# Mixer C's score products: from 128-row stacks of high and low parts to 64-row products of a head's two parts on the two halves of the array's rows

## Chip, cores and metric

The kernel runs on one core of one Trainium2 chip. The metric is the device time of one execution in microseconds; lower is better.

## What is computed

The reference is a two-layer encoder trunk on 1024 tokens of width 1024. Layer 0 mixes by dilated window attention (mixer A) and latent attention (mixer B), layer 1 by differential attention (mixer C). Each layer goes on with a normalisation, a gated feed-forward net with a convolution, and a gated embedding. The change touches mixer C alone, which for each of 8 heads computes two score matrices from two query and two key parts of width 64:

```python
def mixer_c(x, cos_c, sin_c, w_qkv, lam_params, subln, w_out, lambda_init):
    ...
    q = apply_rope(h[..., :C_QK].reshape(B, S, C_HEADS, 2, C_HEAD_DIM), ...)
    k = apply_rope(h[..., C_QK:2 * C_QK].reshape(B, S, C_HEADS, 2, C_HEAD_DIM), ...)
    v = h[..., 2 * C_QK:].reshape(B, S, C_HEADS, 2 * C_HEAD_DIM)
    ...
    s = jnp.einsum("bhcqd,bhckd->bhcqk", qi, kf) * (dh ** -0.5)
    a = jax.nn.softmax(s, axis=-1)
    return jnp.einsum("bhqk,bhkd->bhqd", a[:, :, 0] - lam * a[:, :, 1], vf)
```

The factor dh ** -0.5 is 0.125. The outputs are normalised by head and projected.

## The kernel before

All large products run on TensorE (PE) in the type fp32r. To keep precision, each operand is split into a high part h, which is the value rounded to fp32r, and a low part l, which is the rest; a product is then the sum h*h + h*l + l*h (`mm3`, lines 157 to 160). The high parts are mostly written by ScalarE (ACT) and the low parts by VectorE (DVE, `lo_part`, line 141). GpSimd (POOL) does the rotation of queries and keys (lines 229 to 236), some high parts of weights (line 138), and scalings.

Mixer C goes head by head, and in each head by 8 tiles of 128 queries, so 64 items (`ItemC`, line 815). While a head's items run, the next head is projected, one tile of tokens in each slot (`Block64.project`, line 526). The names in the trace are:

- `pp`: the projection of one token tile to 384 columns (queries, keys, values of one head), 24 matmuls on lines 158 to 160. ACT copies queries and keys to `nat` (line 541) and the values' high part to `v` (line 549), DVE writes the values' low part, POOL rotates `nat` and copies the queries to `q` (line 138).
- `kt`: the transposed keys of one tile (`keys`, line 555, one transpose for both parts). They become `ks`, which holds the high part of a key part in 64 rows and its low part in the other 64: two copies by ACT (line 562) and two subtractions by DVE (line 141), each of 64 rows.
- `qt`: the transposed queries of one tile (`query`, line 565). POOL writes each part twice side by side, PE transposes each of the two doubled parts, ACT multiplies by 0.125 and rounds (line 574), DVE writes the low part (line 575). This is done three items ahead (`prep`).
- `s`: the scores of one part, 128 queries by 1024 keys, in two PSUM banks (`scores`, line 578). Each of two key halves takes two matmuls of 128 rows: high queries against the stack of high and low keys, then low queries against it. There are two such buffers, `bufs=2` in `banks2`, so the two parts of an item hold both.
- DVE takes the negative maximum of each row (`nmx`, line 828); ACT writes the exponentials `e` and their sum `l` (line 438); DVE takes the reciprocal `r` (line 833) and multiplies it by minus lambda for the second part (line 834); POOL scales the first `e` (line 835); DVE adds the second, scaled, to it (line 836).
- `xt`: eight transposes of an item's `e` (line 163), split into `pth` by ACT (line 397) and `ptl` by DVE (line 141), two halves each. After each second item these meet the values in `av`, 24 matmuls.

The loop that sets the order in which this is written is `pipeline` (line 469): in slot i come the scores and softmax of item i + 1 (`a`), the preparation of item i + 3, the slot's step of the plan (a projected tile of the next head, which also transposes the tile before it), the value products of the item before (`c`), and the transposes of item i (`b`):

```python
            if i + 1 < n:
                items[i + 1].a()
            if i + 3 < n:
                items[i + 3].prep()
            plan.run(i, "mid")
```

A scheduler then fixes each engine's order from this and puts in the waits; on the chip each engine runs its own list strictly in that order. Exponentials, split probabilities, keys, values, queries and the transposed input share one pool of 36 buffers of 4 KB in each partition (`unit`, `runit`). Banks of PSUM for `pp`, `kt`, `qt`, `xt` and `av` come from four others (`bank`). In the last slot of a head the weights of the head after next are loaded and split (line 148, `wl`). While the last head's items run, the slots hold weights and products of the following stages (`last_plan`, line 918).

Of the kernel before, what the change touches and what calls it, by code (L numbers as in the profile page):

```python
# [11 lines left out]
AF = mybir.ActivationFunctionType  # L12
ALU = mybir.AluOpType
AX = mybir.AxisListType

P = 128
NT = 8
NK = 8
# [13 lines left out]
def tile_hybrid_encoder(  # L32
# [32 lines left out]
    nc = tc.nc  # L65
# [15 lines left out]
    def runit(s, shape):  # L81
        return unit(s, shape, F32R)

    class Region:

        def __init__(self, kb):
            self.cm = tc.tile_pool(name=nm("rg"), bufs={2: 16, 3: 8, 4: 6}[kb])
            self.pool = self.cm.__enter__()
# [23 lines left out]
    def mid1(s, shape, dt=F32, tag="nat"):  # L112
        return sm.tile(shape, dt, tag=tag, name=nm(s), bufs=3 if tag == "nat" else 2)
# [7 lines left out]
    def bank(s):  # L121
        return ps.tile([P, 512], F32, tag="b", name=nm(s), bufs=4)

    def banks2(s):
        return ps.tile([P, 1024], F32, tag="s", name=nm(s), bufs=2)
# [4 lines left out]
    def blocks(ap):  # L130
        return ap.rearrange("p (k q) -> p k q", q=P)

    def tk(t):
        return slice((t % 4) * P, (t % 4) * P + P)
# [5 lines left out]
    def lo_part(lo, src, hi):  # L140
        nc.vector.tensor_tensor(lo, src, f32(hi), op=ALU.subtract)  # L141
# [15 lines left out]
    def mm3(o, lh, ll, rh, rl, start, stop):  # L157
        nc.tensor.matmul(o, lhsT=lh, rhs=rh, start=start, stop=False)  # L158
        nc.tensor.matmul(o, lhsT=lh, rhs=rl, start=False, stop=False)  # L159
        nc.tensor.matmul(o, lhsT=ll, rhs=rh, start=False, stop=stop)  # L160

    def transpose(o, i):
        nc.tensor.transpose(o, in_=i, identity=ident)  # L163
# [12 lines left out]
    C2a = cp.tile([P, NT, 16], F32, name="C2a")  # L176
# [260 lines left out]
    def exp_rows(dst, s, negmax, l):  # L437
        nc.scalar.activation(dst, s, AF.Exp, bias=negmax, scale=1.0, accum_out=l)  # L438
# [57 lines left out]
    class Block64:  # L496
# [29 lines left out]
        def project(self, t, lag=1):  # L526
            hf = t // 4
            if t % 4 == 0:
                self.ks[hf] = runit("ks", [P, 2, 512])
                self.v[hf] = runit("v", [P, 4, 256])  # L530
                if hf == 0:
                    self.q = unit("q", [P, NT, 2, 64])
            pp = bank("pp")
            for k in range(NK):
                xh, xl = self.xt.tok(k, t)
                wh, wl = self.w[k // 2]
                mm3(pp[:, 0:384], xh, xl, wh[:, k % 2, :], wl[:, k % 2, :], k == 0, k == NK - 1)
            if t >= lag:
                self.keys(t - lag)
            nat = mid1("nat", [P, 4, 64])  # L540
            nc.scalar.copy(nat, pp[:, 0:256].rearrange("p (j d) -> p j d", j=4))
            vt = self.v[hf][:, t % 4, :]
            if self.is_a:
                psv = pp[:, 256:384].rearrange("p (j d) -> p j d", j=2)
                vh = vt.rearrange("p (b d) -> p b d", d=64)[:, 0::3, :]
                vl = vt[:, 64:192].rearrange("p (b d) -> p b d", d=64)
            else:
                psv, vh, vl = pp[:, 256:384], vt[:, 0:128], vt[:, 128:256]
            nc.scalar.copy(vh, psv)
            lo_part(vl, psv, vh)  # L550
            rope(nat[:, :, 0:16], nat[:, :, 0:16], C2a[:, t, :], S2a[:, t, :], 4, 8)
            pool_copy(self.q[:, t], nat[:, 0:2, :])
            self.nat[t] = nat

        def keys(self, t):
            nat = self.nat.pop(t)
            pt = bank("kt")[:, 0:P]
            transpose(pt, nat[:, 2:4, :].rearrange("p j d -> p (j d)"))
            for j in range(2):
                h, l = (slice(0, 64), slice(64, 128)) if j == 0 else (slice(64, 128), slice(0, 64))  # L560
                ks = self.ks[t // 4][:, j, tk(t)]
                nc.scalar.copy(ks[h], pt[h])
                lo_part(ks[l], pt[h], ks[h])
# [11 lines left out]
            nc.vector.scalar_tensor_tensor(qt[:, 1], pt[:, 0:n, :], 0.125, f32(qt[:, 0]), op0=ALU.mult, op1=ALU.subtract)  # L575
            return qt

        def scores(self, qt, i, j):
            s = banks2("s")
            for kh in range(2):  # L580
                for hl in range(2):
                    nc.tensor.matmul(s[:, kh * 512:kh * 512 + 512], lhsT=qt[:, hl, i, :], rhs=self.ks[kh][:, j, :],  # L582
                                     start=hl == 0, stop=hl == 1)
            return s

    class ItemA:
        def __init__(self, blk, j, t, mask, st):
            self.blk, self.j, self.t, self.mask, self.st = blk, j, t, mask, st
# [151 lines left out]
    class Latent:  # L740
# [62 lines left out]
        def turn(self):  # L803
# [8 lines left out]
            nc.scalar.copy(h, pt[:, 0:kk, :])  # L812
            lo_part(l, pt[:, 0:kk, :], h)

    class ItemC:
        def __init__(self, blk, t, st):
            self.blk, self.t, self.st = blk, t, st

        def prep(self):
            self.qt = self.blk.query(self.t, [0, 1])  # L820

        def a(self):
            l = small("l2", [P, 2])
            es = []
            for j in range(2):
                s = self.blk.scores(self.qt, j, j)
                nmx = small("nmx", [P, 1])
                nc.vector.tensor_reduce(out=nmx, in_=s, axis=AX.X, op=ALU.max, negate=True)  # L828
                e = unit("e", [P, 1024])
                exp_rows(e, s, nmx, l[:, j:j + 1])  # L830
                es.append(e)
            r = small("r2", [P, 2])
            nc.vector.reciprocal(r, l)
            nc.vector.tensor_tensor(r[:, 1:2], r[:, 1:2], neglam, op=ALU.mult)
            nc.gpsimd.tensor_scalar(es[0], es[0], r[:, 0:1], 1.0, op0=ALU.mult, op1=ALU.mult)
            nc.vector.scalar_tensor_tensor(es[0], es[1], r[:, 1:2], es[0], op0=ALU.mult, op1=ALU.add)
            self.e = es[0]
# [173 lines left out]
    def mixer_c(xt, late):  # L1011
        new_region(3)
        oT2 = big("oT2", [P, 2, 1024])
        last = {}

        def sink(i):
            def f(oT):
                if i < 7:
                    nc.sync.dma_start(out=mix[1][i], in_=oT)
                last["oT"] = oT  # L1020
            return f
        blk = [Block64(xt, w_c[i], False) for i in range(8)]
        blk[0].load(True)
        for t in range(NT):
            blk[0].project(t, 2)
            if t == 1:
                late()
        blk[0].keys(NT - 2)
        items, plan = [], Plan()
        for i in range(8):  # L1030
            sti = {"sink": sink(i), "oT": oT2[:, i % 2, :] if i < 7 else unit("oT", [P, 1024])}
            items += [ItemC(blk[i], t, sti) for t in range(NT)]
            if i < 7:
                blk[i + 1].plan(plan, 8 * i - 1, 1)
            else:
                w, mt = last_plan(plan, 1, 56, 63)
        plan.add(-1, "first", lambda: blk[0].keys(NT - 1))
        plan.add(-1, "last", lambda: blk[1].load(True), lambda: blk[1].project(0))
        pipeline(items, plan)
        return w, mt, last["oT"]  # L1040
# [469 lines left out]
```

## Time and profile before

| what | value |
|---|---|
| runs | 3137.59, 3142.58 and 3142.8 us; median 3142.58 us |
| profiled execution | 3139.44 us, its span 3137.6 us, mean granted clock of TensorE 0.987 |
| busy, share of the span | PE 96%, weight loads of PE 83%, DVE 73%, ACT 38%, POOL 33% |
| chain that ended last | PE 82%, DVE 9%, DMA 3%, ACT 3%, issue 2%, POOL 2% |
| scores of mixer C, line 582 | 512 matmuls, 3.5% of the chain |

The profile is one execution, taken apart instruction by instruction. A row of a timeline gives start, length, engine, line, operation, the output and input by the program's names, their shapes, and in brackets how long the engine had been idle and what ended that. Matmuls overlap in the array, so the sum of their lengths is more than the time they take; the distance of their starts, or the chain of waits, gives what one costs in a row. A row that ends in "x2" joins two instructions in a row.

### The profile page before, as it was taken

The page shows a single profiled execution, that of the slowest core. Times are in us where ns is not written, and L with a number is a line of the kernel's source. Part 1 is how long each engine was busy: PE and PEld are TensorE (multiplying, and loading weights), DVE is VectorE, ACT ScalarE, POOL GpSimd, SP SyncE. Part 2 cuts the span into 40 slices and gives each one's busy share as a digit, 9 for nine tenths or more (in the row PEclk, how much of TensorE's full clock was granted, in tenths as well). Part 3 has the DMA queues.
Part 4 walks back from the last instruction along what each step waited for, and adds up shares of the span by engine and source line. Part 5 has one row for each costly group of instructions (what it writes and reads, how often), then busy time and mean ns, then how long its engine had stood idle before and what let it go on. Part 6 is the DMA issues. An engine that isn't in the chain of part 4 may idle for free.

```text
span 3137.6 us, 43123 instructions
## 1 busy us (share of the span) xinstructions
PE 3023.3 (96%) x15704; PEld 2590.5 (83%) x15704; DVE 2275.3 (73%) x3864; ACT 1182.2 (38%) x2502; POOL 1048.3 (33%) x1546
## 2 busy tenths in 40 slices
PE   8999999999799999999999999999888999999999
PEld 7888989888588888788889999998666888878887
DVE  6666487875887777766648777777679777767764
ACT  5555577761232222101225555555423222211111
POOL 4444534333422221101225555554333222201112
PEclk9999999999899999999999999999998999999999
DMA  3000100143122221623121100004322222244221
GB/s 119 28 28 25 31 28 8 36 131 124 67 81 81 86 84 67 226 101 108 54 68 31 35 28 28 28 18 134 103 99 68 81 81 81 81 167 141 101 74 67
DMA packets 89251, 237.52 MB, mean 76 GB/s; under 512 B 9040, under 2 KB 32720, under 8 KB 89040
## 3 DMA queue, kind: packets, MB, share of 16 engines
q1 hardware_dynamic: 89040, 234.76, 21.7%
q8 instruction: 125, 2.05, 0.3%
q14 instruction: 86, 0.70, 0.1%
HBM read 179.15 MB, written 55.57 MB: 75 GB/s over the span
## 4 chain that ended last, share of the span: by engine, by line
PE 82%; DVE 9%; DMA 3%; ACT 3%; issue 2%; POOL 2%; SPq 0%; DVEq 0%; ACTq 0%; POOLq 0%
PE pb L159 7%; PE pb L158 7%; PE pb L160 7%; PE xt L163 5%; PE pd L158 5%; PE pd L160 5%; PE pd L159 5%; PE pp L158 4%; PE pp L160 4%; PE pp L159 4%; PE s L582 3%; PE pa L158 3%; PE pa L160 2%; PE pa L159 2%; PE pg L158 2%
## 5 line engine op out<-in xcount | busy, mean ns | idle before, releaser
L158 PE MATMUL pd<-dh,dh 128*128 128x512 f32 x704 | 276.0, 392 | 8.5 <-ACT dh L324 7.5
L141 DVE TENSOR_TENSOR ptl<-xt,pth 128x512 fp32r<-128x512 f32 (+2 forms) x384 | 240.1, 652 | 57.8 <-ACT pth L397 41.3
L160 PE MATMUL pd<-dh,dl 128*128 128x512 f32 x704 | 275.1, 392 | 2.2 <-DVE dl L141 2.1
L1306 DVE TENSOR_TENSOR xn<-xn,pd 128x512 f32<-128x512 f32 x320 | 212.3, 684 | 88.5 <-PE pd L160 87.7
L159 PE MATMUL pd<-dl,dh 128*128 128x512 f32 x704 | 274.9, 391 | 0.0
L158 PE MATMUL pp<-wh,xth 128*128 128x384 f32 x768 | 266.4, 347 | 8.2 <-ACT wh L145 8.0
L159 PE MATMUL pp<-wl,xth 128*128 128x384 f32 x768 | 258.9, 337 | 1.3 <-DVE wl L148 1.3
L160 PE MATMUL pp<-wh,xtl 128*128 128x384 f32 x768 | 258.1, 336 | 0.0
L438 ACT ACTIVATE e<-s,nmx 128x1024 f32<-128x1024 f32 x192 | 214.4, 1118 | 96.6 <-DVE nmx L828 73.8
L158 PE MATMUL pb<-xt,wh 128*128 128x512 f32 x528 | 207.2, 392 | 0.0
L159 PE MATMUL pb<-xt,wh 128*128 128x512 f32 x528 | 206.9, 392 | 0.0
L160 PE MATMUL pb<-xt,wl 128*128 128x512 f32 x528 | 206.9, 392 | 0.0
L324 ACT CAST wh<-ws 128x512 fp32r<-128x512 f32 x132 | 81.7, 620 | 319.9 <-PE pb L159 261.8
L163 PE MATMUL xt<-ident,e 128*128 128x128 f32 x1440 | 194.7, 275 | 5.6 <-POOL e L731 3.0
L138 POOL TENSOR_SCALAR wh<-ws 128x512 fp32r<-128x512 f32 x44 | 29.8, 677 | 458.1 <-PE pa L159 428.8
L163 PEld LDWEIGHTS xt<-ident,e 128*128 128x128 f32 x1440 | 164.4, 141 | 18.7 <-POOL e L731 4.3
L141 DVE TENSOR_TENSOR wl<-ws,wh 128x512 fp32r<-128x512 f32 x176 | 160.8, 914 | 24.1 <-ACT wh L324 23.9
L324 ACT CAST dh<-dr 128x1024 fp32r<-128x1024 f32 x44 | 46.1, 1051 | 346.6 <-DMA dr<-gated 201.9
L138 POOL TENSOR_SCALAR dh<-dr 128x1024 fp32r<-128x1024 f32 x44 | 47.0, 1070 | 367.1 <-DMA dr<-in_w_down_dram 190.7
L158 PEld LDWEIGHTS pd<-dh,dh 128*128 128x128 f32 x704 | 132.9, 189 | 37.8 <-issue 8.3
L160 PEld LDWEIGHTS pd<-dh,dl 128*128 128x128 f32 x704 | 132.5, 188 | 32.9 <-DVE dl L141 5.3
L158 PEld LDWEIGHTS pp<-wh,xth 128*128 128x128 f32 x768 | 144.7, 189 | 13.8 <-ACT wh L145 8.9
(270 smaller groups left out, 8751.0 us busy)
## 6 DMA issues: line engine op xcount, KB each, us to landing
wf<-in_w_gate_dram SPq DMA_DIRECT2D x44, 512.0 KB, 3.2
wf<-in_w_up_dram SPq DMA_DIRECT2D x44, 512.0 KB, 4.2
gated<-c SPq DMA_DIRECT2D x44, 512.0 KB, 2.6
dr<-in_w_down_dram SPq DMA_DIRECT2D x44, 512.0 KB, 3.2
dr<-gated SPq DMA_DIRECT2D x44, 512.0 KB, 4.0
wr<-in_w_c_dram SPq DMA_DIRECT2D x32, 384.0 KB, 3.2
pes<-peo SPq DMA_DIRECT2D x64, 128.0 KB, 2.1
xmid<-xn SPq DMA_DIRECT2D x16, 512.0 KB, 2.9
```

Of the source, the lines that this page charges most:

```text
L138: nc.gpsimd.tensor_scalar(o, i, 1.0, 1.0, op0=ALU.mult, op1=ALU.mult)
L141: nc.vector.tensor_tensor(lo, src, f32(hi), op=ALU.subtract)
L158: nc.tensor.matmul(o, lhsT=lh, rhs=rh, start=start, stop=False)
L159: nc.tensor.matmul(o, lhsT=lh, rhs=rl, start=False, stop=False)
L160: nc.tensor.matmul(o, lhsT=ll, rhs=rh, start=False, stop=stop)
L163: nc.tensor.transpose(o, in_=i, identity=ident)
L324: nc.scalar.copy(h, v)
L438: nc.scalar.activation(dst, s, AF.Exp, bias=negmax, scale=1.0, accum_out=l)
L582: nc.tensor.matmul(s[:, kh * 512:kh * 512 + 512], lhsT=qt[:, hl, i, :], rhs=self.ks[kh][:, j, :], start=hl == 0, stop=hl == 1)
L1306: nc.vector.tensor_tensor(xns[t][:, sl], xns[t][:, sl], po, op=ALU.add)
```

## The change

Mixer C gets a block class of its own, `BlockC`. After the projection, one transpose turns both query parts of a tile and a second one both key parts, so that part 0 lies in rows 0 to 63 and part 1 in rows 64 to 127. ACT writes their high parts in one copy (line 841), DVE their low parts in one subtraction, into `qkh` and `qkl`, which each hold queries and keys of half the tokens. The doubled queries, their copies on POOL, and the queries' own transposes and splits are gone; `prep` is empty. The scores take, for each part and each half of the keys, three matmuls of 64 rows (high by high, high by low, low by high) instead of two of 128, twelve in all, in which the two parts alternate (line 851). The factor 0.125 moves from the query to the softmax: DVE multiplies the negative maximum by it (line 870), and the exponential has it as its scale (line 871).

```diff
+        def keys(self, t):
+            nat = self.nat.pop(t)
+            pt = blocks(bank("kt"))[:, 0:2, :]
+            for i in range(2):
+                transpose(pt[:, i, :], nat[:, 2 * i:2 * i + 2, :].rearrange("p j d -> p (j d)"))
+            h, l = (x[:, :, tk(t)] for x in self.qk[t // 4])
+            nc.scalar.copy(h, pt)
+            lo_part(l, pt, h)
...
-        def scores(self, qt, i, j):
-            s = banks2("s")
-            for kh in range(2):
-                for hl in range(2):
-                    nc.tensor.matmul(s[:, kh * 512:kh * 512 + 512], lhsT=qt[:, hl, i, :], rhs=self.ks[kh][:, j, :],
-                                     start=hl == 0, stop=hl == 1)
-            return s
+        def scores(self, t):
+            ss = [banks2("s") for _ in range(2)]
+            for hf in range(2):
+                for n, (a, b) in enumerate(((0, 0), (0, 1), (1, 0))):
+                    for j, s in enumerate(ss):
+                        half = slice(64 * j, 64 * j + 64)
+                        nc.tensor.matmul(s[:, hf * 512:hf * 512 + 512], lhsT=self.qk[t // 4][a][half, 0, tk(t)],
+                                         rhs=self.qk[hf][b][half, 1, :], start=n == 0, stop=n == 2)
+            return ss
...
         def prep(self):
-            self.qt = self.blk.query(self.t, [0, 1])
+            pass
 
         def a(self):
             l = small("l2", [P, 2])
             es = []
-            for j in range(2):
-                s = self.blk.scores(self.qt, j, j)
+            for j, s in enumerate(self.blk.scores(self.t)):
                 nmx = small("nmx", [P, 1])
                 nc.vector.tensor_reduce(out=nmx, in_=s, axis=AX.X, op=ALU.max, negate=True)
                 e = unit("e", [P, 1024])
-                exp_rows(e, s, nmx, l[:, j:j + 1])
+
+                nc.vector.tensor_scalar(nmx, nmx, 0.125, None, op0=ALU.mult)
+                nc.scalar.activation(e, s, AF.Exp, bias=nmx, scale=0.125, accum_out=l[:, j:j + 1])
                 es.append(e)
...
-        blk = [Block64(xt, w_c[i], False) for i in range(8)]
+        blk = [BlockC(xt, w_c[i]) for i in range(8)]
```

The projection itself is the same as before; its units for a head are now four of `qkh` and `qkl` and two of `v`, where they were two of `ks`, two of `v` and one of `q`.

The order on PE around the scores of an item in the middle of a head, before (`x2` and `x4` join repeated rows):

```order
L163 MATMUL xt_17019<-ident,e_16835 128x128 x4
L163 MATMUL xt_17026<-ident,e_16835 128x128 x4
L582 MATMUL s_17034<-ks_16265,qt_16856 128x512 x2
L582 MATMUL s_17034<-ks_16441,qt_16856 128x512 x2
L582 MATMUL s_17043<-ks_16265,qt_16856 128x512 x2
L582 MATMUL s_17043<-ks_16441,qt_16856 128x512 x2
L163 MATMUL qt_17059<-ident,q_3698_17057 128x128 x2
```

And at such an item now; 16265 and 16435 number the two halves of the tokens in `qkh`, 16266 and 16436 those in `qkl`, and the two tiles `s` are the two parts:

```order
L163 MATMUL xt_16866<-ident,e_16718 128x128 x4
L851 MATMUL s_16874<-qkh_16265 128x512
L851 MATMUL s_16875<-qkh_16265 128x512
L851 MATMUL s_16874<-qkl_16266,qkh_16265 128x512
L851 MATMUL s_16875<-qkl_16266,qkh_16265 128x512
L851 MATMUL s_16874<-qkh_16265,qkl_16266 128x512
L851 MATMUL s_16875<-qkh_16265,qkl_16266 128x512
L851 MATMUL s_16874<-qkh_16435,qkh_16265 128x512
L851 MATMUL s_16875<-qkh_16435,qkh_16265 128x512
L851 MATMUL s_16874<-qkl_16436,qkh_16265 128x512
L851 MATMUL s_16875<-qkl_16436,qkh_16265 128x512
```

Part 0 was complete before part 1 began; now the two alternate to the end, and the query transposes that followed are gone. In this way the parts alternate in 58 of the 64 items.

The order on DVE from the maxima of one item to those of the next, in the middle of a head, before:

```order
L828 TENSOR_REDUCE nmx_17687<-s_17682 128x1
L828 TENSOR_REDUCE nmx_17696<-s_17691 128x1
L575 SCALAR_TENSOR_TENSOR qt_17710<-qt_17707,qt_17710 128x256
L833 RECIPROCAL r_3837_17700<-l_3830_17681 128x2
L834 TENSOR_TENSOR r_3837_17700<-r_3837_17700,neglam 128x1
L836 SCALAR_TENSOR_TENSOR e_17689<-e_17698,r_3837_17700,e_17689 128x1024
L141 TENSOR_TENSOR ks_17523<-kt_17738,ks_17523 64x128
L141 TENSOR_TENSOR v_17524<-pp_17713,v_17524 128x128
L141 TENSOR_TENSOR ptl_17665<-xt_17755,pth_17663 128x4x128
L141 TENSOR_TENSOR ks_17523<-kt_17738,ks_17523 64x128
L141 TENSOR_TENSOR ptl_17666<-xt_17762,pth_17664 128x4x128
L828 TENSOR_REDUCE nmx_17775<-s_17770 128x1
```

And now:

```order
L867 TENSOR_REDUCE nmx_17627<-s_17613 128x1
L867 TENSOR_REDUCE nmx_17632<-s_17614 128x1
L870 TENSOR_SCALAR nmx_17627<-nmx_17627 128x1
L870 TENSOR_SCALAR nmx_17632<-nmx_17632 128x1
L874 RECIPROCAL r_3803_17637<-l_3796_17612 128x2
L875 TENSOR_TENSOR r_3803_17637<-r_3803_17637,neglam 128x1
L141 TENSOR_TENSOR qkl_17460<-kt_17667,qkh_17459 128x2x128
L141 TENSOR_TENSOR v_17461<-pp_17642,v_17461 128x128
L877 SCALAR_TENSOR_TENSOR e_17629<-e_17634,r_3803_17637,e_17629 128x1024
L141 TENSOR_TENSOR ptl_17596<-xt_17682,pth_17594 128x4x128
L141 TENSOR_TENSOR ptl_17597<-xt_17689,pth_17595 128x4x128
```

Both scalings stand behind both maxima, and the low parts of keys, queries and values now stand between the reciprocal and the combination of the two `e`.

The order on DVE at the last item of a head, from its second maximum on, before:

```order
L828 TENSOR_REDUCE nmx_17344<-s_17339 128x1
L575 SCALAR_TENSOR_TENSOR qt_17358<-qt_17355,qt_17358 128x256
L148 TENSOR_TENSOR wl_17406<-wr_17403,wh_17405 128x768
L833 RECIPROCAL r_3758_17348<-l_3751_17329 128x2
L834 TENSOR_TENSOR r_3758_17348<-r_3758_17348,neglam 128x1
```

And now:

```order
L867 TENSOR_REDUCE nmx_17292<-s_17274 128x1
L870 TENSOR_SCALAR nmx_17287<-nmx_17287 128x1
L148 TENSOR_TENSOR wl_17345<-wr_17342,wh_17344 128x768
L870 TENSOR_SCALAR nmx_17292<-nmx_17292 128x1
L874 RECIPROCAL r_3733_17297<-l_3726_17272 128x2
L875 TENSOR_TENSOR r_3733_17297<-r_3733_17297,neglam 128x1
```

The split of a weight stood behind both maxima and ahead of the reciprocal; it now stands between the scalings of the two maxima.

More of the change, by code (lines that the diff above doesn't have):

```diff
@@ L813, in turn, with __init__, project @@
             lo_part(l, pt[:, 0:kk, :], h)
+    class BlockC(Block64):
+        def __init__(self, xt, wdram):
+            Block64.__init__(self, xt, wdram, False)
+            self.qk = [None] * 2
+        def project(self, t, lag=1):
+            hf = t // 4
+            if t % 4 == 0:
+                self.qk[hf] = (runit("qkh", [P, 2, 512]), runit("qkl", [P, 2, 512]))
+                self.v[hf] = runit("v", [P, 4, 256])
+            pp = bank("pp")
+            for k in range(NK):
+                xh, xl = self.xt.tok(k, t)
+                wh, wl = self.w[k // 2]
+                mm3(pp[:, 0:384], xh, xl, wh[:, k % 2, :], wl[:, k % 2, :], k == 0, k == NK - 1)
+            if t >= lag:
+                self.keys(t - lag)
+            nat = mid1("nat", [P, 4, 64])
+            nc.scalar.copy(nat, pp[:, 0:256].rearrange("p (j d) -> p j d", j=4))
+            vh, vl = (self.v[hf][:, t % 4, c] for c in (slice(0, 128), slice(128, 256)))
+            nc.scalar.copy(vh, pp[:, 256:384])
+            lo_part(vl, pp[:, 256:384], vh)
+            rope(nat[:, :, 0:16], nat[:, :, 0:16], C2a[:, t, :], S2a[:, t, :], 4, 8)
+            self.nat[t] = nat
+        def keys(self, t):
[15 more added lines that the diff above has]
+            return ss
     class ItemC:
```

## The prediction

> **What bounds the kernel now.** I read the page's slices first (they place mixer C between about 1610 and 2210 us of the span of 3137.6 us), then the busy time by head in windows, then the chain of waits and each engine's timeline over two query tiles. The windows of one whole head and of the last head:
>
> ```profile
> core 0: us, PE busy (x) PEld busy (x) DVE busy (x) ACT busy (x) POOL busy (x), PEclk, DMA share, GB/s
> 1809.40:1880.40 71.00, 70.00 (x442) 65.86 (x441) 53.62 (x90) 39.26 (x93) 39.19 (x64) 1.00 0.10 31
> 2138.20:2210.00 71.80, 62.85 (x335) 51.71 (x333) 59.51 (x76) 40.97 (x96) 27.44 (x25) 0.95 0.53 163
> ```
>
> A head takes 71.00 us and TensorE (PE) is busy for 70.00 of it, at full clock; only the last head leaves it 9 us of idle time. The chain of waits over two tiles says the same. Its columns are start, length, engine and line:
>
> ```profile
> 1731.14 1.87 PE s L582 x8
> 1733.01 0.22 PE qt L163 x2
> ...
> 1737.42 0.11 PE kt L163
> 1737.53 0.87 PE xt L163 x8
> 1738.40 1.88 PE s L582 x8
> ...
> 1747.66 0.87 PE xt L163 x8
> ```
>
> A tile without value products (1731.14 to 1738.40) takes 7.26 us: scores 1.87, query transposes 0.22, projection 4.19 (1733.23 to 1737.42), key transpose 0.11, transposes of e 0.87. With value products the next scores would start at 1747.66 + 0.87 = 1748.53, 10.13 us after 1738.40. So two tiles take 17.39 us on PE, 8.70 a tile.
>
> But VectorE (DVE) is close behind, and that decides this case. Its timeline over the same tiles, with the exponentials (ACT) and the scaling (POOL) between its steps:
>
> ```profile
> 1732.57 2.35 DVE L828 TENSOR_REDUCE nmx<-s 128x1 f32<-128x1024 f32 x2
> 1734.83 0.41 DVE L575 SCALAR_TENSOR_TENSOR qt<-qt,qt 128x256 fp32r<-128x256 f32 x1
> 1736.18 0.17 DVE L833 RECIPROCAL r<-l 128x2 f32<-128x2 f32 x1 [0.94 <-ACT e L438]
> ...
> 1737.61 1.29 DVE L836 SCALAR_TENSOR_TENSOR e<-e,r,e 128x1024 f32<-128x1024 f32 x1 [1.07 <-POOL e L835]
> 1738.93 0.28 DVE L141 TENSOR_TENSOR ks<-kt,ks 64x128 fp32r<-64x128 f32 x1
> ...
> 1739.46 0.68 DVE L141 TENSOR_TENSOR ptl<-xt,pth 128x512 fp32r<-128x512 f32 x1
> 1740.17 0.29 DVE L141 TENSOR_TENSOR ks<-kt,ks 64x128 fp32r<-64x128 f32 x1
> 1740.49 0.69 DVE L141 TENSOR_TENSOR ptl<-xt,pth 128x512 fp32r<-128x512 f32 x1
> 1741.10 2.34 DVE L828 TENSOR_REDUCE nmx<-s 128x1 f32<-128x1024 f32 x2
> ...
> 1748.76 1.29 DVE L141 TENSOR_TENSOR ptl<-xt,pth 128x512 fp32r<-128x512 f32 x2 [0.94 <-ACT pth L397]
> 1749.96 1.21 DVE L828 TENSOR_REDUCE nmx<-s 128x1 f32<-128x1024 f32 x1
> ```
> ```profile
> 1733.81 1.12 ACT L438 ACTIVATE e<-s,nmx 128x1024 f32<-128x1024 f32 x1 [0.16 <-DVE nmx L828]
> ...
> 1734.94 1.12 ACT L438 ACTIVATE e<-s,nmx 128x1024 f32<-128x1024 f32 x1
> ```
> ```profile
> 1736.45 1.13 POOL L835 TENSOR_SCALAR e<-e,r 128x1024 f32<-128x1024 f32 x1 [2.73 <-DVE r L833]
> ```
>
> This is a ring that DVE runs in strict order: two maxima, wait for the exponentials, reciprocal, wait for POOL, combine (L836), low parts, next maxima. From 1732.57 to 1741.10 it takes 8.53 us with no other wait in it. In the next tile, 8.86 us, it waits 0.94 us for PE (through pth). So PE bounds now, and the ring has only about 0.9 us to spare in two tiles. What matters is that the first exponential starts at 1733.81, while the second maximum still runs: the exponentials overlap the maxima.
>
> **The change part by part.**
>
> *Scores.* Eight matmuls of 128 rows go, twelve of 64 rows come, in pairs on the two row halves. No 64-row matmul stands in the trace; the nearest rows:
>
> ```profile
> L582 PE MATMUL s<-ks,qt 128*128 128x512 f32 x512 | 141.4, 411 | 3.8 <-DVE ks L141 1.6 <-ACT e L438 1.3 <-ACT qt L574 0.9
> ...
> L160 PE MATMUL s<-kh,qt 96*128 96x512 f32 x128 | 52.1, 407 | 0.0
> ```
>
> A 96-row product lasts as long as a 128-row one (407 against 411 ns), so fewer rows alone save nothing. In a row, eight take 1.87 us, 0.234 each. Bounds for the group of twelve: 6 x 0.234 = 1.40 us if the halves of a pair run at once, 12 x 0.234 = 2.81 if one after the other. I take 1.40, since the halves share neither rows nor output tile. Entering and leaving the 64-row form may cost something; a matmul lasts 411 ns but gives way to the next after 234, so emptying the array is bounded by 0.18 us a switch, 0 to 0.36 a tile. The query transposes go (0.22), a second transpose beside the keys' comes (0.11). PE then needs 8.70 - 1.87 - 0.22 + 1.40 + 0.11 = 8.12 us a tile, up to 8.48 with the switches.
>
> The Trainium skill's page "TensorE: Matmul & The Clock Gate", Part 3, says that matmuls on distinct row groups run at the same time with starts some 4 ns apart, which is the 1.40 us; no run here shows it yet. Against the change speaks "TensorEngine Tiling (Array Packing)", Tiling Modes: changing the mode drains the array; by it the 8.48 would hold, without it the 8.12.
>
> *The scaling of the maximum.* The query is no longer multiplied by 0.125, so a DVE instruction scales each maximum, and each exponential waits for it. The built order puts both behind the second maximum. So the first exponential no longer overlaps that. The nearest row for the new instruction and its hand-over is mixer A's 128x1 step, by group and in the timelines of DVE and ACT:
>
> ```profile
> L610 DVE TENSOR_SCALAR nmx<-mx 128x1 f32<-128x1 f32 x64 | 13.0, 204 | 0.0
> ```
> ```profile
> 105.68 0.21 DVE L610 TENSOR_SCALAR nmx<-mx 128x1 f32<-128x1 f32 x1
> ```
> ```profile
> 106.01 0.94 ACT L438 ACTIVATE e<-e,nmx 128x768 f32<-128x768 f32 x1 [1.46 <-DVE nmx L610]
> ```
>
> That is 0.21 us and 0.12 until the exponential starts, 0.33 at most (0.17, a reciprocal's length, at least); I take 0.31. The new ring: two maxima 2.26 (1732.57 to 1734.83), scaling 0.31, two exponentials until the reciprocal 2.37 (1733.81 to 1736.18), until the combining 1.43, until the low parts 1.32, both low parts 1.20 (1748.76 to 1749.96): 8.89 us. The low parts of queries, keys and values (L575, L141) that stood in the old ring cost nothing there: what is left of them now stands before the combining, inside its wait of 1.07 us for POOL. If that cover went, they would cost 0.6 us a tile. So the ring (8.89) is longer than PE's tile (8.12 to 8.48) and than the old 8.70. PE's saving becomes PE's waiting, and PE may lose 0.4 to 0.8 us a tile more without any effect.
>
> *The end of a head.* The last tile's ring, where the next weights are split, and the first of the next head:
>
> ```profile
> 1704.94 2.35 DVE L828 TENSOR_REDUCE nmx<-s 128x1 f32<-128x1024 f32 x2
> ...
> 1707.54 2.35 DVE L148 TENSOR_TENSOR wl<-wr,wh 128x768 fp32r<-128x768 f32 x1
> 1709.81 0.15 DVE L833 RECIPROCAL r<-l 128x2 f32<-128x2 f32 x1
> ...
> 1716.95 2.35 DVE L828 TENSOR_REDUCE nmx<-s 128x1 f32<-128x1024 f32 x2
> ...
> 1723.26 1.21 DVE L828 TENSOR_REDUCE nmx<-s 128x1 f32<-128x1024 f32 x1
> ```
> ```profile
> 1710.07 1.12 POOL L835 TENSOR_SCALAR e<-e,r 128x1024 f32<-128x1024 f32 x1 [0.99 <-DVE r L833]
> ...
> 1712.96 0.32 POOL L236 TENSOR_TENSOR nat<-rope,rope 128x64 f32<-128x64 f32 x1
> ```
> ```profile
> 1713.33 0.33 PE L163 MATMUL kt<-ident,nat 128*128 128x128 f32 x1 [1.00 <-POOL nat L236]
> ```
>
> Here PE already waits 1.00 us for the rotated keys, which stand on POOL behind the scaling of e. The weight split (2.27 us, 1707.54 to 1709.81) now stands between the two scalings, so the second exponential and all behind it start after it: 2.26 + 0.21 + 2.27 + 0.31 + 1.24 (1734.94 to 1736.18) = 6.29 us to the reciprocal instead of 4.87. Then 0.26 to POOL, 3.21 until the rotation ends (1710.07 to 1713.28), 0.44 for two transposes, about 1.5 for scores whose second half waits for these keys: 11.7 us until the next head's first maxima. Before it was 12.01, since transposes stood among the scores. The first tile then needs 2.26 + 0.31 + 2.37 + 1.43 + 1.32 = 7.69 instead of 6.31 (1716.95 to 1723.26).
>
> *Off the path.* Two POOL copies a tile, one ACT and one DVE step on keys and one each on queries go; none ends a wait in the ring. A head holds six 4 KB units of the common pool instead of five; in the built order no step of the ring waits for another engine's old use of such a unit, so I cost it at nothing; a wait there would add to the ring.
>
> **The sum.** A head: 6 x 8.89 + 11.7 + 7.69 = 72.7 us against 71.0, 1.7 more. Six whole heads give 10.4. For the rest of the first head I add 2, an estimate from the ring against its tiles. In the last head the shortest items go from 7.68 to about 8.9:
>
> ```profile
> 2188.51 2.34 DVE L828 TENSOR_REDUCE nmx<-s 128x1 f32<-128x1024 f32 x2
> ...
> 2196.19 2.34 DVE L828 TENSOR_REDUCE nmx<-s 128x1 f32<-128x1024 f32 x2
> ```
>
> Its other items are longer, among loads of output weights (163 GB/s in its window), and can take up part of this; I add 3, an estimate. Together 15 us. The profiled execution took 3139.44 us (the span and 1.84 around it), the runs shown 3137.59 to 3142.8 with a median of 3142.58. So 3154.8 by the one and 3158 by the other; I take 3156. With 0.17 for the scaling and nothing in the part heads it would be 6 us, with 1 us more at each head's end about 22.
>
> **The rivals.**
>
> *The pairs don't overlap.* PE's tile becomes 8.70 - 2.09 + 2.81 + 0.11 = 9.53 us, with switches 9.89, above the ring. That is 6.6 to 9.5 us a head, 46 to 67 over seven, and up to 7 in the last: 3186 to 3213, about 3198. For it: no row shows two matmuls at once. Against it: nothing is shared by a pair. It also covers the case that the change does not do what it says. Chance 0.11.
>
> *PE stays the bound and keeps its gain.* If the exponentials still overlapped enough for the ring to stay under 8.12, each tile would gain 8.70 - 8.12 = 0.58 us, 4.6 a head, about 33 in all with the last: 3109; with the switches at 0.36 about 13: 3129. It decides from the ring's falling below 8.70. For it: PE's 70.00 of 71.00. Against it: the old ring already took 8.53 in the tile at 1732.57, and the new order only lengthens it. Chance 0.07.
>
> *The forecast*, the ring bounds: chance 0.82.
>
> **How the numbers follow.** The ring's own bounds give 3145 to 3165. The range 3142 to 3175 takes these with the spread of the runs and more at the heads' ends; it leaves out the faster rival and the one without overlap, 0.18. A measurement can tell about 0.2%, 6.3 us, from no change. Faster has the second rival's 0.07; the forecast's low end lies within 6.3 us, some 0.13; the rest, 0.80, is slower.
>
> **What would show it.** Right: in a middle head PE's busy time falls below 66 us of 72 to 73; maxima start 8.8 to 8.9 us apart; the first exponential starts about 1.4 us later after its maximum's start than the 1.24 of now; a group of twelve matmuls takes 1.3 to 1.8 us. Wrong: a group of 2.6 us or more with PE still over 95% busy (no overlap), or heads of 68 us or less with PE busy throughout (the ring is shorter than I say).

## The result and the profile after

The changed kernel took 3160.83 us in the median of four runs (3158.03 to 3161.63), the kernel before 3141.32 in four runs beside it. The ratio is 1.0067, with a 95% interval of 1.0055 to 1.008: 0.67% slower, some 20 us. The profiled execution's span is 3156.0 us, against 3137.6, so the two traces account for 18.4 us. The mean granted clock of TensorE (PE) fell from 0.987 to 0.983.

Where the 18.4 us are, from the starts of the maxima (a head is counted from its first maximum to that of the next) and, for the end, from the first output step behind the mixer (line 1066 before, 1107 after):

| stretch | before, us | after, us | difference |
|---|---|---|---|
| up to the first maximum | 1650.01 | 1649.60 | -0.4 |
| first head | 66.94 | 71.64 | +4.7 |
| next six heads together | 425.61 | 435.08 | +9.5 |
| last head, to its last item's maxima | 62.71 | 63.21 | +0.5 |
| last item, to the first output step | 20.45 | 23.68 | +3.2 |
| the rest of the kernel | 911.9 | 912.8 | +0.9 |

The six whole heads are not alike. The windows of two of them, after:

```profile
core 0: us, PE busy (x) PEld busy (x) DVE busy (x) ACT busy (x) POOL busy (x), PEclk, DMA share, GB/s
1794.59:1865.96 71.37, 68.85 (x465) 62.02 (x466) 49.26 (x90) 33.97 (x76) 32.53 (x47) 1.00 0.09 30
1937.32:2010.15 72.83, 70.31 (x465) 62.91 (x466) 49.27 (x90) 33.99 (x76) 35.27 (x50) 0.97 0.09 30
```

Two heads run at full clock and take 71.37 and 71.36 us, only 0.4 more than before (71.00). The other four take 72.4 to 73.8, at a granted clock of 0.96 to 0.97. So there are two losses here, and the second is not in the prediction.

**The ring.** VectorE's (DVE) steps over one tile in the middle of a head:

```profile
1747.38 2.34 DVE L867 TENSOR_REDUCE nmx<-s 128x1 f32<-128x1024 f32 x2
1749.64 0.26 DVE L870 TENSOR_SCALAR nmx<-nmx 128x1 f32<-128x1 f32 x2
1752.21 0.17 DVE L874 RECIPROCAL r<-l 128x2 f32<-128x2 f32 x1 [2.30 <-ACT e L871]
...
1753.64 1.34 DVE L877 SCALAR_TENSOR_TENSOR e<-e,r,e 128x1024 f32<-128x1024 f32 x1 [0.44 <-POOL e L876]
1754.90 1.28 DVE L141 TENSOR_TENSOR ptl<-xt,pth 128x512 fp32r<-128x512 f32 x2
1756.10 2.34 DVE L867 TENSOR_REDUCE nmx<-s 128x1 f32<-128x1024 f32 x2
```

And ScalarE's (ACT) first exponential of that tile:

```profile
1749.87 1.12 ACT L871 ACTIVATE e<-s,nmx 128x1024 f32<-128x1024 f32 x1 [4.72 <-DVE nmx L870]
```

Maxima start 8.72 us apart, and DVE has no wait for PE in between. In a head at full clock the eight tiles take 7.48, 9.27, five times 8.70 to 8.75, and 11.00 us, so this ring is the tile in five of the eight. The first exponential starts 2.49 us after its maximum began; before it was 1.24. That is the ring the prediction spoke of.

**PE.** The chain of waits after, with the scores of three tiles in a row (the lengths are distances to the next step):

```profile
1743.18 0.87 PE xt L163 x8
1744.06 1.60 PE s L851 x12
1745.65 0.38 PE pp L158
...
1754.00 1.59 PE s L851 x12
...
1761.05 1.59 PE s L851 x9
```

Two tiles take 1761.05 - 1744.06 = 16.99 us, 8.50 a tile: less than DVE's 8.72, and 0.2 less than PE's own 8.70 before. Since scores for the next tile may run ahead of DVE, PE does not show the difference tile by tile; it collects until the end of the head.

**The end of a head.** There PE waits for the rotated keys. PE's rows there in a head at full clock and in a slowed one:

```profile
1863.83 0.44 PE L163 MATMUL kt<-ident,nat 128*128 128x128 f32 x2 [2.12 <-POOL nat L236]
1864.20 0.50 PE L851 MATMUL s<-qkh 64*128 64x512 f32 x2
```
```profile
1791.16 0.69 PE L163 MATMUL kt<-ident,nat 128*128 128x128 f32 x2 [2.12 <-POOL nat L236]
1791.78 0.79 PE L851 MATMUL s<-qkh 64*128 64x512 f32 x2
```

The wait has grown from 1.00 to 2.12 us in both. Behind it the same rows are longer in the second, 0.69 against 0.44 us. The granted clock around that place, in windows of 3.4 us:

```profile
1787.40:1790.80 3.40, 1.21 (x10) 0.74 (x7) 2.70 (x6) 2.25 (x8) 2.82 (x5) 1.00 0.66 224
1790.80:1794.20 3.40, 3.04 (x14) 2.10 (x14) 1.21 (x3) 0.37 (x1) 3.32 (x4) 0.50 0.01 2
1794.20:1797.60 3.40, 3.40 (x25) 3.12 (x22) 3.01 (x6) 1.64 (x3) 2.25 (x2) 0.99 0.45 125
```

PE was busy for 1.21 of 3.4 us, then gets half its clock for 3.4 us, just when the next head's scores stand on the path, then all of it again. This happens at five of the seven changes of head (once for 6.8 us). In the trace of before it happens at none of them; in mixer C it is found there only later, in the last head.

### The profile page after: what moved, and what is told of

The parts are those of the page before. It is cut to its first block, busy times and chain, and to the rows that moved or that the text cites. A ratio compares the mean times of both kernels' runs of the same rounds, so it can differ in the third digit from the quotient of the medians.

```text
span 3156.0 us, 43260 instructions
## 1 busy us (share of the span) xinstructions
PE 3030.3 (96%) x15896; PEld 2574.5 (82%) x15896; DVE 2237.8 (71%) x3864; ACT 1142.0 (36%) x2374; POOL 1003.7 (32%) x1418
## 5 line engine op out<-in xcount | busy, mean ns | idle before, releaser
L871 ACT ACTIVATE e<-s,nmx 128x1024 f32<-128x1024 f32 x128 | 141.8, 1113 | 233.4 <-DVE nmx L870 186.0
L876 POOL TENSOR_SCALAR e<-e,r 128x1024 f32<-128x1024 f32 x64 | 73.9, 1155 | 304.4 <-DVE r L874 304.4
```

Of the source, the lines that this page charges most:

```text
L871: nc.scalar.activation(e, s, AF.Exp, bias=nmx, scale=0.125, accum_out=l[:, j:j + 1])
```

## The experiments

All ratios are to the kernel before, run on the same chip beside each. Theory 1 was: the delayed exponentials make DVE's ring the tile, and PE's longer wait at a head's end halves its clock. Its first rival was that the 64-row products are what costs.

**The scaling taken out of the softmax** (changed kernel):

```diff
-            nc.scalar.copy(nat, pp[:, 0:256].rearrange("p (j d) -> p j d", j=4))
+            nc.scalar.activation(nat[:, 0:2], pp[:, 0:128].rearrange("p (j d) -> p j d", j=2), AF.Copy, scale=0.125)
+            nc.scalar.copy(nat[:, 2:4], pp[:, 128:256].rearrange("p (j d) -> p j d", j=2))
...
-                nc.vector.tensor_scalar(nmx, nmx, 0.125, None, op0=ALU.mult)
-                nc.scalar.activation(e, s, AF.Exp, bias=nmx, scale=0.125, accum_out=l[:, j:j + 1])
+                exp_rows(e, s, nmx, l[:, j:j + 1])
```

> The 0.125 is put into ScalarE's copy of the projected queries (two copies of 128 columns in place of one of 256), and the VectorE step on each maximum goes; the exponentials follow their maxima again. Theory 1 (the exponentials that wait for both maxima and both scalings make VectorE's ring of 8.72 us the tile, and the long wait of PE for the rotated keys at a head's end halves its clock): the first exponential starts about 1.2 us after its maximum started (now 2.49), the ring falls to about 7.5 us, PE's own 8.51 us become the tile, a head about 69.5 us (now 71.4 at full clock, 72.5 in the mean; before 71.0), the whole about 3130 us; with the half clock still there at each head's end about 3138. Theory 2 (the 64-row products themselves are what costs, through the switches of form): nothing changes on PE, a head stays above 71 us and the whole above 3150 us.

Measured: 3133.55 us, ratio 0.9981 (0.9972 to 0.999). A whole head, by window:

```profile
1855.74:1925.73 69.99, 68.76 (x465) 61.78 (x466) 48.28 (x73) 35.42 (x84) 33.34 (x47) 1.00 0.10 31
```

It takes 70.0 us at full clock, 1.0 less than before and 2.5 less than the mean of the changed kernel. The first exponential starts 1.25 us after its maximum again. The 64-row products are the same as in the changed kernel: they are not what costs.

**The scaling moved to ACT** (changed kernel):

```diff
-                nc.vector.tensor_scalar(nmx, nmx, 0.125, None, op0=ALU.mult)
+                nc.scalar.activation(nmx, nmx, AF.Copy, scale=0.125)
```

> The scaling of each maximum stays, but ScalarE does it right before the exponential in place of VectorE. Theory 1 (what costs is that the scaling stands behind the second maximum on VectorE, not that there is one): first exponential about 1.6 us after its maximum started (now 2.49), ring about 7.9 us, so PE's 8.51 us are the tile and the whole is about 3132 us (3140 with the half clock). Rival (any further step between maximum and exponential costs its length, wherever it stands): ring about 8.7 us and the whole about 3160 us.

Measured: 3129.9 us, ratio 0.9969 (0.9958 to 0.9981), the fastest of all and faster than both kernels. Two rows of DVE's timeline and a head's window:

```profile
1825.63 2.34 DVE L867 TENSOR_REDUCE nmx<-s 128x1 f32<-128x1024 f32 x2
1829.67 0.17 DVE L874 RECIPROCAL r<-l 128x2 f32<-128x2 f32 x1 [1.70 <-ACT e L871]
```
```profile
1852.88:1922.02 69.14, 68.23 (x465) 61.86 (x466) 48.65 (x74) 37.63 (x92) 33.80 (x48) 1.00 0.10 31
```

The reciprocal comes 4.04 us after the maximum began (4.83 in the changed kernel), though each exponential still has a scaling ahead of it, 0.20 us on ACT. Tiles now take 8.13 and 8.86 us in turn, 8.50 in the mean, which is PE's own time. So it was the place behind the second maximum that cost, not the step. The first exponential no longer waits for the second maximum, and PE bounds again.

**The scaling alone, in the kernel before** (queries multiplied by 1.0, otherwise as before):

```diff
-            self.qt = self.blk.query(self.t, [0, 1])
+            self.qt = self.blk.query(self.t, [0, 1], 1.0)
...
-                exp_rows(e, s, nmx, l[:, j:j + 1])
+                nc.vector.tensor_scalar(nmx, nmx, 0.125, None, op0=ALU.mult)
+                nc.scalar.activation(e, s, AF.Exp, bias=nmx, scale=0.125, accum_out=l[:, j:j + 1])
```

> The kernel before, with its 128-row scores, its query transposes and copies, and of the change only the scaling: queries are no longer multiplied by 0.125, VectorE scales each maximum and the exponential scales the scores. Theory 1: the first exponential starts about 2.5 us after its maximum (before 1.24), the ring of a tile reaches about 8.7 us, which is PE's own 8.70, so the tiles barely change, but at a head's end PE waits 1.5 to 2 us for the rotated keys (before 1.00), a head takes 71.5 to 72 us, and the whole is 3 to 6 us above the kernel before, 8 to 14 if the waits halve the clock. Rival (the loss needs the 64-row products, the scaling alone costs nothing): within 2 us of the kernel before.

Measured: 3157.87 us, ratio 1.0062 (1.005 to 1.0074): nearly the whole loss of the change, without any of its 64-row products. The amount was missed; 3 to 6 us had been expected, 8 to 14 with a halved clock. DVE's rows and a head's window:

```profile
1827.54 2.35 DVE L828 TENSOR_REDUCE nmx<-s 128x1 f32<-128x1024 f32 x2
...
1832.37 0.17 DVE L834 RECIPROCAL r<-l 128x2 f32<-128x2 f32 x1 [2.04 <-ACT e L831]
...
1836.31 2.35 DVE L828 TENSOR_REDUCE nmx<-s 128x1 f32<-128x1024 f32 x2
...
1845.62 2.35 DVE L828 TENSOR_REDUCE nmx<-s 128x1 f32<-128x1024 f32 x2
```
```profile
1866.20:1938.90 72.70, 70.65 (x441) 65.72 (x440) 56.55 (x105) 38.98 (x92) 38.84 (x64) 1.00 0.09 30
```

The reciprocal comes 4.83 us after the maximum, as in the changed kernel. But here the tiles take 8.77 and 9.31 us: the two low parts of keys and the one of values a tile, which the new layout shortens, do not all fit into DVE's wait for GpSimd (POOL). The head is 72.7 us at full clock; PE's wait at its end stays at 1.1 us. So the loss has the same cause as in the changed kernel but not the same shares: a whole head loses 1.7 us at full clock here, 0.4 there, where the halved clock adds the rest.

**Two orders of the twelve products** (changed kernel), three and three, then six and six:

```diff
-                for n, (a, b) in enumerate(((0, 0), (0, 1), (1, 0))):
-                    for j, s in enumerate(ss):
-                        half = slice(64 * j, 64 * j + 64)
+                for j, s in enumerate(ss):
+                    half = slice(64 * j, 64 * j + 64)
+                    for n, (a, b) in enumerate(((0, 0), (0, 1), (1, 0))):
```

> The twelve products of a tile in the order six of one part, six of the other (in each half of the columns three and three), with no other change. If two neighbours on the two row halves run at once (theory 1), the group now grows from 1.60 to about 3.0 us (12 x 0.234 and the two switches), PE's tile from 8.51 to about 9.8 us, above the ring of 8.72; a head about 78 us, the whole 3195 to 3215 us, and PE without waits in the middle of a head. If the order does not matter (products of different row halves overlap over a distance, or never do), the group stays at 1.60 us and the whole at about 3161 us.

```diff
-            for hf in range(2):
-                for n, (a, b) in enumerate(((0, 0), (0, 1), (1, 0))):
-                    for j, s in enumerate(ss):
-                        half = slice(64 * j, 64 * j + 64)
+            for j, s in enumerate(ss):
+                half = slice(64 * j, 64 * j + 64)
+                for hf in range(2):
+                    for n, (a, b) in enumerate(((0, 0), (0, 1), (1, 0))):
```

> The order in a tile is all six products of one part, then all six of the other. With three and three the group still took 1.60 us. If the second half of the rows can start while up to six products of the first half stand ahead of it, the group stays at 1.60 us and the whole at about 3157 us. If the reach is shorter than six products, part of the overlap goes: group 2 to 3 us, PE's tile above the ring of 8.72 us, the whole 3165 to 3210 us. The first part's maximum could also start earlier, by up to 0.7 us, if the two parts ran one after the other.

Measured for three and three: 3156.14 us, ratio 1.0053 (1.0035 to 1.0071), so theory 1's 3195 to 3215 us fell. PE's rows, from the first of the group to the projection behind it:

```profile
1869.84 0.50 PE L851 MATMUL s<-qkh 64*128 64x512 f32 x2
...
1871.44 0.45 PE L158 MATMUL pp<-wh,xth 128*128 128x384 f32 x1
```

The group still takes 1.60 us, and its first row joins the first product of both parts, though two others stand between them in the program. The built order is three and three too, in 52 of the 64 items, so it is not the scheduler that pairs them. PE did not start its list strictly in order here, though "The kernel before" says that of every engine. Measured for six and six: 3160.92 us, ratio 1.007 (1.0052 to 1.0088). PE's rows:

```profile
1870.60 0.50 PE L851 MATMUL s<-qkh 64*128 64x512 f32 x1
1870.93 0.39 PE L851 MATMUL s<-qkl,qkh 64*128 64x512 f32 x1
1871.16 0.39 PE L851 MATMUL s<-qkh,qkl 64*128 64x512 f32 x1
1871.17 0.49 PE L851 MATMUL s<-qkh 64*128 64x512 f32 x1
...
1872.75 0.44 PE L158 MATMUL pp<-wh,xth 128*128 128x384 f32 x1
```

Now the second part starts 0.57 us later, with the first part's third product, and the group takes 2.15 us. So the second half of the rows started past three waiting products of the first half, not past four or five. The tile grows by the same 0.55 us, to 9.06 in the mean (8.94 and 9.18 in turn), above the ring of 8.72. The whole is no slower than the changed kernel all the same, and no halved clock stands at a change of head in its profile: PE, now the bound, waits only 0.82 us there (1863.14), except at the first change (2.12).

**All twelve products on one half of the rows** (changed kernel):

```diff
-                        half = slice(64 * j, 64 * j + 64)
+                        half = slice(0, 64)
```

> Both parts' twelve products use the operands of the first part, so that all sit on the same half of the array's rows (the second part's scores are left out, the first part's are computed twice). Order, sizes and count stay. If a pair in the changed kernel runs at once on two halves (0.234 us a pair), the group now takes about 2.8 us and 0.4 of switches (1.60 and 0.2 in the changed kernel), PE's tile 9.7 us, a head about 77 to 79 us, the whole about 3200 to 3215 us. If a 64-row product simply takes half as long as a 128-row one (0.117 us each, one after the other), nothing changes: group 1.60 us, whole about 3157 us.

Measured: 3204.96 us, ratio 1.021 (1.0192 to 1.0228). PE's rows of a group, and a head:

```profile
1888.39 0.73 PE L851 MATMUL s<-qkh 64*128 64x512 f32 x2
...
1891.34 0.44 PE L158 MATMUL pp<-wh,xth 128*128 128x384 f32 x1
```
```profile
1883.05:1962.46 79.41, 78.95 (x465) 70.50 (x464) 49.59 (x90) 34.44 (x76) 34.39 (x48) 1.00 0.09 27
```

The group takes 2.95 us, and tiles 8.73 and 10.96 in turn, 9.84 in the mean. A 64-row product alone is as long as a 128-row one (0.23 us in a row); the 1.60 us come from two at once.

**PE's wait at a head's end filled with idle work** (changed kernel):

```diff
+            if t == NT - 1:
+                for i in range(18):
+                    transpose(pb[:, 2 + i % 2, :], ident)
```

> Before the last tile's transposes of a head's rotated queries and keys stand 18 transposes of the identity into the unused half of the same bank: about 1.9 us of work that nothing reads, in the wait of 2.12 us. If the halved clock at the starts of five heads comes from PE's waiting there (theory 1), the clock stays at 1.00, the scores at a head's start take 1.6 us instead of 2.7, heads that took 72.4 to 73.8 us take about 71.4, and the whole falls by about 8 us to 3152 us, though the work grows. If the halved clock has another cause (a limit on power or the 64-row form), the dips stay and the whole is 3161 us or up to 1 us more.

Measured: 3148.6 us, ratio 1.0035 (1.0024 to 1.0047). PE's rows at a change of head and a head's window:

```profile
1929.99 2.13 PE L163 MATMUL kt<-ident 128*128 128x128 f32 x18
1932.27 0.44 PE L163 MATMUL kt<-ident,nat 128*128 128x128 f32 x2 [0.15 <-POOL nat L236]
1932.64 0.50 PE L855 MATMUL s<-qkh 64*128 64x512 f32 x2
```
```profile
1934.40:2005.74 71.34, 70.80 (x483) 63.96 (x484) 49.28 (x89) 33.97 (x76) 33.76 (x48) 1.00 0.10 31
```

Five heads in a row take 71.34 to 71.37 us at a clock of 1.00, 6.0 us less together than in the changed kernel. Only at the seventh change, where PE now waits 2.76 us in the middle of the scores (at 2150.31), a halved stretch is left. Work that nothing reads made the kernel some 10 us faster (1.0067 to 1.0035). That shows that the halved clock followed from PE's idling, and what it cost in these heads. The trace is still 8.9 us longer than that of before. Only 1.7 of these lie in the five heads at full clock; the first head has 3.8, and the one before the seventh change, with the long wait and the halved stretch, 3.9.

**Half of that filling** (9 transposes in place of 18):

> As the filled wait, with 9 transposes of the identity in place of 18: PE still waits about 1.1 us for the rotated keys at a head's end (2.12 in the changed kernel, 0.15 with 18). If the half clock comes from the length of PE's idle time, this is as short as in the kernel before (1.00 us), which had no halved clock: no dips, whole about 3149 us as with 18. If any wait there sets it off, some dips come back: 3152 to 3160 us.

Measured: 3154.09 us, ratio 1.0045 (1.0033 to 1.0057), between the two. The profiled run, 3149.6 us, shows waits of 1.1 us and no halved clock at the first six changes of head, as with 18. But it is the fastest of its five runs, which reach up to 3156.07, and nothing shows what the others did there; their mean clocks, 0.985 to 0.987, do not tell them apart. Its profile speaks for the length of the idle time; its times are inconclusive.

**The last weight split given to POOL**, in the changed kernel and in the version with the scaling on ACT:

```diff
+        def load_part(self, i, idle):
+            if idle:
+                return Block64.load_part(self, i, idle)
+            self.w.append(load_split(self.wdram[:, 2 * i:2 * i + 2, :], [P, 2, 384], "w", rtile, nc.gpsimd, nc.gpsimd))
```

> The changed kernel, with the one weight split per head that VectorE still did between the two scalings of the last tile (1.64 to 2.35 us) given to GpSimd like the other three. Theory 1 (part of the lost time at a head's end is this split, and PE's wait there sets off the halved clock): the reciprocal of the last tile comes 4.85 us after its maximum started (now 5.36), the next head's first maximum 10.5 us after it at full clock (now 11.00), PE's wait for the rotated keys falls from 2.12 to about 1.6 us; 0.5 us a head, 3 to 4 us in all, so 3157, and down to 3148 if the shorter wait halves the clock less often. Rival (the four splits in a row on GpSimd, 5.4 us, end after the reciprocal and hold the scaling of e back): nothing gained, 3161 us or above.

> The scaling on ScalarE right before each exponential, and the weight split on GpSimd: both changes together. The first alone took 3130 us, with PE waiting 0.90 us at a head's end. Theory 1: the split's 0.56 us there (reciprocal 4.62 us after the maximum in the last tile, 4.06 in the others) goes, PE's wait falls to about 0.4 us, a head from 69.1 to 68.6 us, the whole to about 3126 us. Rival (GpSimd ends its splits too late): the wait grows instead, by up to 0.8 us a head, 3130 to 3136 us.

Measured: 3156.31 us, ratio 1.0053 (1.004 to 1.0065), and 3132.46 us, ratio 0.998 (0.9971 to 0.9989). The reciprocal did come 4.83 us after the last maxima, as expected. But PE's wait grew, to 2.8 us in the first and 1.6 in the second. POOL's rows there:

```profile
1786.27 0.25 POOL L231 TENSOR_TENSOR rope<-nat,S2a 128x32 f32<-128x32 f32 x1
1786.49 0.83 POOL L138 TENSOR_SCALAR wh<-wr 128x768 fp32r<-128x768 f32 x1
1787.29 0.31 POOL L236 TENSOR_TENSOR nat<-rope,rope 128x64 f32<-128x64 f32 x1
```

In the first, a copy of weights has moved ahead of the last step of the rotation that PE waits for; the 0.5 us gained on DVE are lost on POOL. The next head's first maxima come 11.17 us after the last ones at full clock, against 11.00. The clock was halved at only two of the seven changes of head, although the wait was longest (2.8 us at six of them): above some length, that length alone does not decide it; the last section shows what does. So the 3157 us expected of the first came out, but not for the reason given: PE's wait did not shrink, the clock was halved less often. Of the second version only the longer wait is known; a head takes 69.84 us in it, 0.7 more than with the split on DVE, at full clock.

## Why the prediction came out as it did

It forecast 3156 us and slower, and 3160.83 came. The cause that it named is the right one: the late scaling makes DVE's ring longer than PE's tile and hides the gain of the 64-row pairs. That the sum came so close is luck all the same, since its terms agree less well than it does.

- *The pairs run at once.* Right. The group takes 1.60 us against 1.40 taken; with both on one half it takes 2.95. The Trainium skill's page "TensorE: Matmul & The Clock Gate", Part 3, said so, and the runs agree.
- *The switches of form.* The bound was 0 to 0.36 us a tile. The group is 0.20 longer than 1.40 and the first projection product behind it takes 0.38 us instead of 0.18: 0.40 together. PE's tile is 8.50, against 8.12 to 8.48 forecast. What the Trainium skill's page "TensorEngine Tiling (Array Packing)", Tiling Modes, says of the drain at a change of mode fits this cost, and the sum with the upper bound was the nearer one.
- *The ring.* Right in mechanism, 0.17 too long: 8.72 instead of 8.89. The first exponential starts at 2.49 instead of 2.57, it is 2.34 to the reciprocal instead of 2.37, and the combining takes 1.26 instead of 1.32. It was counted for six tiles, but the second of a head takes 9.27. (With 0.17 for the scaling the prediction gave 6 us as its low end; 0.14 less in each of 48 tiles makes that 3.7.)
- *PE's saving becomes waiting.* Right, but it shows elsewhere: "PE's busy time falls below 66 us of 72 to 73" was wrong. It is 68.85 of 71.37, because PE's tile is only 0.2 shorter and what it saves collects at the head's end. "0.4 to 0.8 us a tile more without any effect" was too generous: it is 0.2.
- *The end of a head.* 11.7 was forecast from the last item's maxima to the next head's; at full clock it is 11.00. The weight split between the two scalings took 1.6 us in place of 2.27, so the reciprocal comes 5.36 us after the maximum (1782.27 to 1787.63), not 6.29:

```profile
1782.27 2.34 DVE L867 TENSOR_REDUCE nmx<-s 128x1 f32<-128x1024 f32 x2
1784.53 0.14 DVE L870 TENSOR_SCALAR nmx<-nmx 128x1 f32<-128x1 f32 x1
1784.59 1.64 DVE L148 TENSOR_TENSOR wl<-wr,wh 128x768 fp32r<-128x768 f32 x1
1786.15 0.14 DVE L870 TENSOR_SCALAR nmx<-nmx 128x1 f32<-128x1 f32 x1
1787.63 0.17 DVE L874 RECIPROCAL r<-l 128x2 f32<-128x2 f32 x1 [1.33 <-ACT e L871]
```

- *The step that failed: a head at full clock.* The sum of 72.7 us a head looks right beside the mean of 72.5 (435.08 / 6). But at full clock a head is 71.37, so six heads would have lost 2.6 us (6 x 71.37 - 425.61), not 10.4: the head's end was put 0.7 us too long, the six middle tiles 0.45 together (52.89 against 53.34), the first tile 0.2 (7.48 against 7.69). The other 6.9 of the 9.5 come from the halved clock, for which the prediction had no term; with PE's wait filled, 6.0 of them were gone in the first five of these heads. It saw PE wait 1.00 us at that place and made the chain up to the rotated keys longer, but did not ask what the longer idle time does to PE itself. Two errors of opposite sign met.
- *The ends.* For the first head 2 was estimated, 4.3 came (with the 0.4 us by which it starts earlier): its first four tiles took 28.9 us before, with PE busy for 65.94 us in that head against 70.00 in the next. They now take 33.6, the first 7.5 instead of 3.8 and the others the ring's 8.7. For the last head 3 was estimated. Its items lost 0.5, but the last of all lost 3.2: its second scaling stands behind another weight split, and its exponentials start 1.6 and 2.0 us after their scalings, behind other steps of ACT (lines 890, 933 and 936). PE's clock is halved in part of that time too, 0.83 in the mean of the window. DVE's and ACT's rows there, and the window:

```profile
2219.53 2.35 DVE L867 TENSOR_REDUCE nmx<-s 128x1 f32<-128x1024 f32 x2
...
2222.98 0.15 DVE L870 TENSOR_SCALAR nmx<-nmx 128x1 f32<-128x1 f32 x1
2226.38 0.17 DVE L874 RECIPROCAL r<-l 128x2 f32<-128x2 f32 x1 [3.26 <-ACT e L871]
```
```profile
2223.48 1.11 ACT L871 ACTIVATE e<-s,nmx 128x1024 f32<-128x1024 f32 x1
...
2225.14 1.12 ACT L871 ACTIVATE e<-s,nmx 128x1024 f32<-128x1024 f32 x1
```
```profile
2219.53:2243.21 23.68, 19.13 (x95) 16.11 (x95) 13.62 (x23) 14.66 (x34) 3.99 (x6) 0.83 0.30 98
```

The reciprocal comes 6.85 us after the maximum; in the kernel before it was 3.86 (2205.27 to 2209.13). That both losses follow the scaling, the experiments show. With the scaling alone in the kernel before, the first head takes 71.39 us and the last item 23.29; with the scaling on ACT they take 65.95 and 20.73, where the kernel before has 66.94 and 20.45. The shares of the single steps are read from the traces; no experiment took them apart.

Both rivals were built in the end. Without overlap the kernel takes 3205 us with tiles of 9.84 (forecast 3198, 9.53 to 9.89). With the exponentials ahead of the second maximum PE bounds and it takes 3130 (forecast 3129 with the switches).

## What to carry to other kernels

A cheap step on a per-row statistic costs little by its length and much by its place: behind the second of two maxima it undoes an overlap between two engines, and one line that puts it on the consumer's engine gave the gain back. Where two engines' tiles are within a few per cent (8.70 and 8.53 here), follow both rings to the end before counting a saving on either. And where a saving on PE turns into waiting, look at how long PE idles in one piece, since that can slow the work behind it.

## What the runs showed of the hardware

- One wait of 2.12 us (with 0.4 to 0.5 us just ahead of it) was enough to halve PE's granted clock, at five of seven changes of head, and at four of seven in the order three and three. Each stretch lasted 3.4 us, two of them 6.8. With waits of 0.9 to 1.6 us there (the kernel before, the scaling on ACT, with POOL's split too) no profile shows one; with 2.8 us it is two of six. The Trainium skill's page "TensorE: Matmul & The Clock Gate", Part 1, tells of a window of 3.4 us that runs freely and does not start with the work. The traces agree: in each of them all halved stretches start whole multiples of 3.413 us apart, to within some 5 ns, so they lie on one grid of windows. Before a halved stretch at these changes of head PE was busy for 0.99 to 1.59 us of such a window (changed kernel, three and three), or 0.60 and 1.46 (POOL's split alone). Around the waits that no halved stretch followed it was busy for 1.59 us or more in both windows that the wait touches. So it goes by the place of the wait on this grid, as far as these traces show; no run moved a wait there on purpose. The edge at 1862.51 cuts one wait of 2.12 us in two, and that leaves 2.22 us of work before it and 2.10 behind it, at full clock. The window before it, its columns as in the heads' windows above:

```profile
1859.10:1862.51 3.41, 2.22 (x18) 1.74 (x16) 1.73 (x5) 3.23 (x8) 1.93 (x3) 1.00 0.71 227
```

The line is not sharp in busy time as the profile gives it: with half of the filling, a window with 1.80 us at the seventh change was followed by a halved one too.

- Products on the second half of the array's rows started past up to three waiting products of the first half (three and three: 1.60 us as in the alternating order; six and six: 0.57 us late).
- DVE's weight split took 1.64 us at the end of a head in the changed kernel and 2.35 in the kernel before, on the same shapes. POOL ran a split of its own beside it for 0.8 us in the first (until 1785.42) and for 1.5 us in the second (1778.54 to 1780.06); that this is the cause was not tried.
